# Down projections of a two-layer decoder step: where the residual rows, the first pair's weights and the last group's tiles are asked for

## The chip, the core and the metric

The kernel runs on one core of one Trainium2 chip. The metric is the time of one execution on the device in microseconds (us); before the change it is 2305.55 us, the median of three runs (2301.43, 2305.55 and 2307.38). Engines are called as the profile calls them: PE (TensorE's matmuls; PEld are its weight loads), DVE (VectorE), ACT (ScalarE), POOL (GpSimd) and SP (SyncE), which here only issues DMAs, one after the other in a fixed order.

## The reference, cut to what matters

A decoder of two layers works on 1024 prompt rows and 64 sample rows, 1088 columns in the kernel's layout (features lie on the partitions). Each layer is a mixer and a gated feed-forward block (FFN), and the change lies in the end of the FFN, its down projection:

```python
def _conv_ffn(h, buf, w_up, conv_w, conv_b, w_down):
    z = h @ w_up
    zc, new_buf = _causal_dwconv(z, buf, conv_w, conv_b)
    g, u = jnp.split(zc, 2, axis=-1)
    return (jax.nn.gelu(g) * u) @ w_down, new_buf
...
        y, fb = _conv_ffn(hn, ffn_buf[l], p['w_ffn_up'][l], p['ffn_conv_w'][l], p['ffn_conv_b'][l], p['w_ffn_down'][l])
        new_ffn.append(fb.astype(x.dtype))
        x = x + y
```

`w_ffn_down` is 2816 x 1024: 22 tiles of 128 inner features and 8 tiles of 128 output features. The last line is the residual add.

## The kernel before, in words

Every fp32 product is made of three matmuls on two-part numbers: each operand is split into a high part (made by ACT, a rounding copy) and a low part (made by DVE, value less high part), and PE adds high x high, high x low and low x high (`mm3`).

The residual `X` (8 rows of 128 x 1088, one row for each output tile) is written to DRAM ahead of the FFN (`self.spill`, "spf" in the profile), because the FFN's up projection uses the place of `X` for its own rows: four rows `Zs`, two rows `Ys` and the product row `YG`. The 22 finished inner tiles go to DRAM too (`yd`). The down projection fetches both again. It has three groups of inner tiles, `GROUPS = (6, 8, 8)`:

- **Group 0** (tiles 0 to 5) lies in the buffer `HX` and is multiplied directly: `first_block(w, m, o, n)` makes output tile m for a block of columns, on one of five PSUM banks, and DVE adds it to the residual row. Tiles m = 0, 1, 2 go block by block, then m = 3 and 4, each over the three blocks `TB`; then m = 5, 6, 7 together over the four blocks `QB` of 136 columns in either half. So PE has left the columns 0 to 271 of `HX` (the first two of the four blocks) half way through that last part. For each block `first_block` fetches the residual's piece from DRAM into a buffer of the pool `tmpp` ("xr").
- **Group 1** (tiles 6 to 13) is multiplied by a seven-product scheme: output tiles in four pairs (m, m + 4), seven products a pair on sums and differences of the operands. Columns go in two blocks, here called the first halves (columns 0 to 271 of either half of the row, `sb` = 0) and the second halves (272 to 543, `sb` = 1). In a pair PE makes four products of the first halves (`dfour`), four of the second, then the three others of each (`dthree`); in the first pair it makes all seven of the first halves and then all seven of the second. Products read by turns from `HB` and from `HX`. `into_hb(k, sb)` fills `HB` (one fetched tile each); `into_hx(k, sb)` fills `HX` for k = 0 to 3 from two fetched tiles y and z: three subtractions or additions on DVE (L727 to L729), then high and low parts (L712 and L713). `HX` still holds group 0, so `into_hx(k, 0)` must wait until PE has left those columns there, `into_hx(k, 1)` until group 0 ends. The seven weights of a pair are made by ACT and DVE from two fetched raw tiles; `W.make()` makes the next one of the seven (`Pair.steps`, L190 to L208). They lie in a pool of ten places, six of which the tiles 5 to 7 of group 0 hold to their end.
- **Group 2** (tiles 14 to 21) is multiplied directly from `HB` again, tile m = 0 over the blocks `TB`. `fetch(f, sb, hi, lo)` brings a tile's half into a buffer of `tmpp` and splits it into `HB` (L638 to L640), once the seven-product scheme has left that part of `HB`; `last(sb)` calls it during the last pair's `dthree`.

What sets the order: `tmpp` has four buffers, which go round among the pieces "xr" and the fetched tiles "yl". A DMA into a buffer is issued by SP when the buffer's last user has ended, and all DMAs stand in one SP queue, so a DMA that waits for a buffer holds back all behind it. A scheduler places the instructions of each engine ahead of time; each engine then takes its own in that order.

Of the kernel before, what the change touches and what calls it, by code (L numbers as in the profile page):

```python
# [11 lines left out]
ALU = mybir.AluOpType  # L12
# [3 lines left out]
KD = 8  # L16
# [72 lines left out]
def hybrid_step(ctx: ExitStack, tc: tile.TileContext, I, O):  # L89
    nc = tc.nc  # L90
# [16 lines left out]
    X = big.tile([P, KD, NT], F32, name="X")  # L107
# [57 lines left out]
    def get_w(key, ahead=4):  # L165
        i = state["next"]
        assert ORDER[i] == key, (ORDER[i], key)
        state["next"] += 1
        load_to(i + 1 + ahead)
        return wtiles.pop(i)  # L170
# [79 lines left out]
    def mm3(out, w_hi, w_lo, x_hi, x_lo, start, stop, more=False):  # L250
        mm(out, w_hi, x_hi, start, False, more)
        mm(out, w_hi, x_lo, False, False, more)
        mm(out, w_lo, x_hi, False, stop, more)
# [11 lines left out]
    def halves(ap, o, n):  # L265

        if len(ap.shape) == 2:
            return ap.rearrange("p (h c) -> p h c", h=2)[:, :, o:o + n]
        return ap.rearrange("p k (h c) -> p k h c", h=2)[:, :, :, o:o + n]

    def mm_halves(w, acts, o, n):

        ps = mmp.tile([P, 512], F32, tag="mm", name="mm")
        out = ps[:, :2 * n].rearrange("p (h c) -> p h c", h=2)
        for k, (hi, lo) in enumerate(acts):
            mm3(out, w[k][:, 0], w[k][:, 1], halves(hi, o, n), halves(lo, o, n), k == 0, k == len(acts) - 1)
        return out

    def blocks(w):
        return [t[:, :, k] for t in w for k in range(4)]  # L280
# [159 lines left out]
    HACTS = [(HH[:, k], HL[:, k]) for k in range(KD)]  # L440
# [40 lines left out]
    class FFN:  # L481
# [22 lines left out]
        def run(self, norm_next, final):  # L504
# [7 lines left out]
            c = 4 * NE  # L512
# [7 lines left out]
            v = nc.vector  # L520

            AF_ = [HX[:, e].rearrange("p q k c -> p (q k c)") for e in (0, 1)]
            AACTS = [tuple(a[:, q * NT:(q + 1) * NT] for a in AF_) for q in range(GROUPS[0])]
# [109 lines left out]
            def fetch(f, sb, hi, lo):  # L633

                o, n = SB[sb]
                t = tmpp.tile([P, 576], F32, tag="tmp", name="yl")
                tv = t[:, :2 * n].rearrange("p (h c) -> p h c", h=2)
                nc.sync.dma_start(tv, halves(self.yd[f], o, n))  # L638
                nc.scalar.activation(halves(hi, o, n), tv, AF.Copy)
                v.tensor_tensor(halves(lo, o, n), tv, halves(hi, o, n).bitcast(F32), ALU.subtract)  # L640

            W = self.first
            W.make(8)
            flush_all_but_last()
            for p in range(NFF):
# [8 lines left out]
                def make(i):  # L654
                    if nxt:
                        nxt.make()

                def make_first(i):
                    if i < 3:
                        make(i)  # L660

                def last(sb):
                    def go(i):
                        if not nxt and sb == 0:
                            q = i - 4
                            fetch(q, 0, *AACTS[q])
                        elif not nxt:
                            for q in {4: (3,), 5: (), 6: (4, 5)}[i]:
                                fetch(q, 0, *AACTS[q])
                    return go  # L670
# [15 lines left out]
                W = nxt  # L686
# [8 lines left out]


            def first_block(w, m, o, n):
                t = tmpp.tile([P, 576], F32, tag="tmp", name="xr")
                tv = t[:, :2 * n].rearrange("p (h c) -> p h c", h=2)
                nc.sync.dma_start(tv, self.spill[:, m, :, o:o + n])  # L700
                ps = mm_halves(blocks(w), AACTS, o, n)
                v.tensor_tensor(halves(X[:, m], o, n), tv, ps, ALU.add)

            def rows(f, sb):
                o, n = SB[sb]
                t = tmpp.tile([P, 576], F32, tag="tmp", name="yl")
                tv = t[:, :2 * n].rearrange("p (h c) -> p h c", h=2)
                nc.sync.dma_start(tv, halves(self.yd[f], o, n))
                return tv

            def put(hi, lo, src):
                nc.scalar.activation(hi, src, AF.Copy)  # L712
                v.tensor_tensor(lo, src, hi.bitcast(F32), ALU.subtract)  # L713

            G0, G1 = GROUPS[0], GROUPS[0] + GROUPS[1]

            def into_hb(k, sb):
                o, n = SB[sb]
                y = rows(G0 + k, sb)
                if k < 4:  # L720
                    v.tensor_tensor(y[:, 1], y[:, 1], y[:, 0], ALU.subtract)  # L721
                put(halves(HH[:, k], o, n), halves(HL[:, k], o, n), y)

            def into_hx(k, sb):
                o, n = SB[sb]
                y, z = rows(G0 + k, sb), rows(G0 + 4 + k, sb)
                v.tensor_tensor(y[:, 1], z[:, 1], y[:, 1], ALU.subtract)  # L727
                v.tensor_tensor(y[:, 0], y[:, 0], y[:, 1], ALU.add)
                v.tensor_tensor(z[:, 0], z[:, 0], y[:, 0], ALU.subtract)  # L729
                put(HX[:, 0, 0:2, k, o:o + n], HX[:, 1, 0:2, k, o:o + n], y)  # L730
                put(HX[:, 0, 2, k, o:o + n], HX[:, 1, 2, k, o:o + n], z[:, 0])

            def dn_pair(m):
                return Pair(self.up, [(key, (1, m)), (key, (1, m + 4))])

            todo = [(k, sb) for sb in (0, 1) for k in range(KD)]
            ws = [get_w((key, (0, m)), ahead=3 - m) for m in range(3)]
            for b in range(3):
                for m in range(3):
                    first_block(ws[m], m, *TB[b])  # L740
                    if b and todo:
                        into_hb(*todo.pop(0))
            for m in (3, 4):
                w = get_w((key, (0, m)), ahead=3)
                for b in range(3):
                    first_block(w, m, *TB[b])
                    into_hb(*todo.pop(0))
            ws = [get_w((key, (0, m)), ahead=KD - 1 - m) for m in (5, 6, 7)]
            W = dn_pair(0)
            for b in range(4):  # L750
                for w, m in zip(ws, (5, 6, 7)):
                    first_block(w, m, *QB[b])
                    if b < 2:
                        if todo:
                            into_hb(*todo.pop(0))
                    elif m > 5:
                        into_hx(2 * (b - 2) + m - 6, 0)
                    if b:
                        W.make({1: 1, 2: 0, 3: 0}[b])
            assert not todo  # L760
            W.make()
            for k in range(4):
                into_hx(k, 1)
                W.make()
# [29 lines left out]
            def dthree(m, W, sb, after):  # L794
                o, n = SB[sb]
                for i, ps, r, c in zip((4, 5, 6), xb.pop(sb), (m, m + 4, m), (o, o, NH + o)):
                    product(W.w[i], i, sb, ps, False)
                    xm = X[:, r, c:c + n]
                    v.tensor_tensor(xm, xm, ps[:, :n], ALU.add)
                    after(i)  # L800

            pair[0] = 1
            for m in range(4):
                nxt = dn_pair(m + 1) if m < 3 else None

                def make(i):
                    if nxt:
                        nxt.make()

                def make_first(i):  # L810
                    if i < 3:
                        make(i)

                def last(sb):
                    def go(i):
                        if nxt:
                            return
                        if sb == 0:
                            for q in (2 * (i - 4), 2 * (i - 4) + 1):
                                if q < 4:  # L820
                                    fetch(G1 + q, 0, *HACTS[q])
                        elif i < 6:
                            for q in (2 * i - 4, 2 * i - 3):
                                fetch(G1 + q, 0, *HACTS[q])
                    return go

                if m:
                    dfour(m, W, 0, make_first)
                    dfour(m, W, 1, make)
                    if not nxt:  # L830
                        load_to(state["next"] + 1)
                    dthree(m, W, 0, last(0))
                    dthree(m, W, 1, last(1))
                else:
                    dfour(m, W, 0, nothing)
                    W.make(8)
                    dthree(m, W, 0, nothing)
                    dfour(m, W, 1, make)
                    dthree(m, W, 1, make)
                W = nxt  # L840
            for q in range(KD):
                fetch(G1 + q, 1, *HACTS[q])

            def down(w, acts, t):
# [7 lines left out]
            for m in range(4):  # L852
                w = get_w((key, (2, m)), ahead=3)
# [678 lines left out]
```

## Time and profile before

| | before |
|---|---|
| median of three runs | 2305.55 us |
| the profiled execution, its time | 2306.45 us |
| its span, first to last instruction | 2304.7 us |
| mean granted TensorE clock | 0.987 |
| PE busy | 2249.4 us, 98% of the span |
| DVE busy | 1758.2 us, 76% |
| ACT busy | 1051.4 us, 46% |
| first layer: group 0, group 1 | 964.7 to 1036.5, 1036.5 to 1132.0 us |
| second layer: group 0, group 1 | 2028.4 to 2100.3, 2100.3 to 2195.5 us |

How to read it: a busy PE is not a PE at its peak, since the ends of matmuls are modelled; a wait shorter than a matmul hides in the busy time, and so does a lowered clock. Stages are therefore best measured from start to start of the same instruction. A row of the timeline has start, length, engine, line, operation, what it writes and reads, how many of the kind, and in brackets the idle time ahead of it and what ended that. A row of the busy times by stretch has the stretch, its length, then busy time and count of PE, PEld, DVE, ACT and POOL, the granted clock, the busy share of the DMA engines and GB/s.

### The profile page before, as it was taken

What the parts mean: (1) busy time and instruction counts of PE and PEld (TensorE: products, weight loads), DVE (VectorE), ACT (ScalarE), POOL (GpSimd) and SP (SyncE); (2) the same over time, 40 slices, a digit from 0 to 9 for tenths busy, and PEclk for the clock granted to TensorE, in tenths of its full rate; (3) what the DMA queues carried; (4) which work ended last, traced back from release to release, by engine and by line L of the source; (5) the groups of instructions that cost most, each with busy time, mean ns of one, the idle gap of its engine ahead of it and who ended that gap; (6) DMA issues with size and microseconds to landing.
All of it is one profiled execution on the core that took longest, in us unless ns stands there. A gap on an engine that the chain in (4) does not pass through costs nothing.

```text
span 2304.7 us, 39660 instructions
## 1 busy us (share of the span) xinstructions
PE 2249.4 (98%) x15992; PEld 2215.4 (96%) x15992; DVE 1758.2 (76%) x3185; ACT 1051.4 (46%) x2144; POOL 36.1 (2%) x65
## 2 busy tenths in 40 slices
PE   9999999989999999998999999998999999998998
PEld 8999998979999999998999999998999999998998
DVE  6899975698888888858737766589888888876745
ACT  6344437445444444523425766434444444533322
POOL 0000000000000000000000121000000000000000
PEclk9999999989999999999999999998999999999999
DMA  5212113212222122464422111322221222265312
GB/s 197 70 39 69 44 55 106 74 58 95 85 85 79 63 84 82 145 175 140 134 74 105 38 37 46 120 79 74 99 81 62 84 85 75 68 219 156 116 59 78
DMA packets 135288, 209.39 MB, mean 91 GB/s; under 512 B 27776, under 2 KB 101888, under 8 KB 134976
## 3 DMA queue, kind: packets, MB, share of 16 engines
q1 hardware_dynamic: 135104, 206.85, 28.3%
q8 instruction: 125, 2.05, 0.4%
q14 instruction: 59, 0.48, 0.1%
HBM read 160.62 MB, written 46.21 MB: 90 GB/s over the span
## 4 chain that ended last, share of the span: by engine, by line
PE 88%; DVE 6%; DMA 3%; ACT 2%; issue 1%; SPq 0%; DVEq 0%; ACTq 0%
PE mm L245 67%; PE ax L245 17%; DMA yl<-yd 2%; DVE acc L371 1%; DVE xe L1261 0%; PE ax L1376 0%; PE ax L1061 0%; DVE ws L160 0%; DVE ws L190 0%; PE ax L1052 0%; DMA X<-in_x 0%; DVE td L411 0%; DVE HB L406 0%; PE ax L1043 0%; PE ax L1023 0%
## 5 line engine op out<-in xcount | busy, mean ns | idle before, releaser
L245 PE MATMUL mm<-HB,ws 128*128 128x272 f32 (+6 forms) x9000 | 1405.0, 310 | 9.0 <-ACT HB L405 2.9
L245 PEld LDWEIGHTS mm<-HB,ws 128*128 128x128 f32 x9000 | 1330.5, 190 | 21.4 <-issue 6.7
L245 PE MATMUL mm<-HX,ws 128*128 128x272 f32 (+3 forms) x2844 | 411.6, 298 | 15.0 <-ACT HX L712 11.4
L245 PEld LDWEIGHTS mm<-HX,ws 128*128 128x128 f32 x2844 | 392.5, 191 | 17.3 <-ACT HX L712 12.3
L124 ACT ACTIVATE ws<-raw 128x512 fp32r<-128x512 f32 x484 | 296.3, 619 | 241.4 <-PE mm L245 113.2
L190 DVE TENSOR_TENSOR ws<-raw,ws 128x512 fp32r<-128x512 f32 x312 | 213.8, 688 | 77.4 <-ACT ws L124 75.0
L245 PE MATMUL ax<-HX,ws 128*128 128x272 f32 (+1 forms) x1872 | 265.1, 290 | 0.8 <-ACT HX L712 0.8
L245 PEld LDWEIGHTS ax<-HX,ws 128*128 128x128 f32 x1872 | 247.6, 189 | 1.6 <-ACT HX L712 1.3
L245 PE MATMUL ax<-HB,ws 128*128 128x272 f32 (+1 forms) x1248 | 171.6, 287 | 0.0
L245 PEld LDWEIGHTS ax<-HB,ws 128*128 128x128 f32 x1248 | 161.8, 188 | 0.0
L929 DVE SCALAR_TENSOR_TENSOR X<-U,par,X 128x1024 f32<-128x1024 f32 x120 | 151.7, 1279 | 0.0
L160 DVE TENSOR_TENSOR ws<-raw,ws 128x512 fp32r<-128x512 f32 (+1 forms) x172 | 110.8, 663 | 49.9 <-ACT ws L124 49.3
L607 ACT ACTIVATE X<-mm 128x272 f32<-128x272 f32 (+1 forms) x88 | 35.1, 398 | 189.6 <-PE mm L245 189.6
L620 DVE SCALAR_TENSOR_TENSOR X<-X,par 128x1104 f32<-128x1104 f32 x88 | 120.1, 1365 | 0.5 <-ACT X L619 0.4
L621 DVE SCALAR_TENSOR_TENSOR X<-X,par 128x1104 f32<-128x1104 f32 x88 | 116.5, 1364 | 0.0
L619 ACT ACTIVATE X<-X,par 128x1104 f32<-128x1104 f32 x88 | 114.2, 1298 | 0.2
L287 DVE TENSOR_TENSOR X<-X,mm 128x384 f32<-128x384 f32 (+1 forms) x66 | 34.6, 530 | 77.8 <-PE mm L245 69.4
L626 ACT ACTIVATE X<-X 128x1024 f32<-128x1024 f32 x44 | 46.6, 1060 | 45.5 <-DVE X L621 45.5
L551 ACT ACTIVATE X<-fst 128x16 f32<-128x16 f32 x88 | 17.9, 212 | 98.6 <-DVE X L621 98.6
L303 ACT ACTIVATE sq<-X 128x384 f32<-128x384 f32 (+1 forms) x42 | 20.7, 504 | 85.0 <-DVE X L287 79.2
L629 DVE TENSOR_TENSOR X<-X 128x1024 f32<-128x1024 f32 x44 | 53.6, 1219 | 0.4
L712 ACT ACTIVATE HB<-yl 128x544 fp32r<-128x544 f32 x32 | 21.0, 658 | 72.1 <-DVE yl L721 41.4
(262 smaller groups left out, 2079.6 us busy)
## 6 DMA issues: line engine op xcount, KB each, us to landing
raw<-in_w SPq DMA_DIRECT2D x176, 512.0 KB, 4.0
yl<-yd SPq DMA_DIRECT2D x120, 272.0 KB, 3.6
yd<-X SPq DMA_DIRECT2D x44, 544.0 KB, 2.7
raw<-in_w SPq DMA_DIRECT2D x16, 384.0 KB, 4.3
spf<-X SPq DMA_DIRECT2D x4, 1152.0 KB, 5.7
xr<-spf SPq DMA_DIRECT2D x20, 208.0 KB, 3.1
X<-in_xt SPq DMA_DIRECT2D x8, 512.0 KB, 6.7
spf<-X SPq DMA_DIRECT2D x4, 1024.0 KB, 5.3
```

Source lines behind the costliest of these rows:

```text
L124: nc.scalar.activation(hi, src, AF.Copy)
L160: nc.vector.tensor_tensor(lo, src, hi.bitcast(F32), ALU.subtract)
L190: nc.vector.tensor_tensor(lo, src, hi.bitcast(F32), ALU.subtract)
L245: nc.tensor.matmul(out, lhsT, rhs, start=start, stop=stop, skip_group_check=more)
L287: nc.vector.tensor_tensor(X[:, m, t0:t0 + n], X[:, m, t0:t0 + n], ps[:, :n], ALU.add)
L607: nc.scalar.activation(low(z1, sb), p1[:, :n], AF.Copy)
L619: nc.scalar.activation(y, z[:, 2:NE], AF.Identity, bias=pc(fb, f), scale=pc(fw, 2 * 44 + f))
L620: v.scalar_tensor_tensor(y, z[:, 1:NE - 1], pc(fw, 44 + f), y, ALU.mult, ALU.add)
L621: v.scalar_tensor_tensor(y, z[:, 0:NE - 2], pc(fw, f), y, ALU.mult, ALU.add)
L626: nc.scalar.activation(YG[:, :NP], y[:, :NP], AF.Gelu_apprx_tanh)
L629: v.tensor_tensor(YG[:, :NP], YG[:, :NP], y[:, :NP], ALU.mult)
L929: nc.vector.scalar_tensor_tensor(cv, U[i][:, j:j + NP], wj, cv, ALU.mult, ALU.add)
```

## The change

Three edits, all in `FFN.run`, so both layers have them.

1. The residual rows of output tiles 3 to 7 no longer pass through `tmpp`. Five DMAs fetch whole rows straight into `X` (rows 3 and 4 at the second block of the tiles 0 to 2, rows 5 to 7 at the third), and `first_block` adds the product to `X` in place. The pieces "xr" stay for m = 0, 1, 2: nine for each layer where there were 27.
2. The first pair's weights: of the eight calls of `W.make()`, two now stand at block 1, one at block 2 and one at block 3 of the tiles 5 to 7, and four with the second halves. Before, three stood at block 1, one behind block 3 and four with the second halves.
3. Group 2: four half tiles (0 to 3 of the second halves) are fetched during the last pair's `dthree` instead of behind it, two at each of its ends.

```diff
             def first_block(w, m, o, n):
+                if m > 2:
+                    ps = mm_halves(blocks(w), AACTS, o, n)
+                    v.tensor_tensor(halves(X[:, m], o, n), halves(X[:, m], o, n), ps, ALU.add)
+                    return
                 t = tmpp.tile([P, 576], F32, tag="tmp", name="xr")
...
             for b in range(3):
+
+                for m in ((), (3, 4), (5, 6, 7))[b]:
+                    nc.sync.dma_start(X[:, m].rearrange("p (h c) -> p h c", h=2), self.spill[:, m])
                 for m in range(3):
...
                     first_block(w, m, *QB[b])
-                    if b < 2:
-                        if todo:
-                            into_hb(*todo.pop(0))
-                    elif m > 5:
+                    if todo:
+                        into_hb(*todo.pop(0))
+                    elif b == 1 or m == 5:
+                        W.make()
+                    else:
                         into_hx(2 * (b - 2) + m - 6, 0)
-                    if b:
-                        W.make({1: 1, 2: 0, 3: 0}[b])
             assert not todo
-            W.make()
...
-                        if sb == 0:
-                            for q in (2 * (i - 4), 2 * (i - 4) + 1):
-                                if q < 4:
-                                    fetch(G1 + q, 0, *HACTS[q])
-                        elif i < 6:
-                            for q in (2 * i - 4, 2 * i - 3):
-                                fetch(G1 + q, 0, *HACTS[q])
+
+                        for q, c in ({4: ((0, 0), (1, 0)), 5: ((2, 0), (3, 0)), 6: ((0, 1), (1, 1))},
+                                     {4: ((4, 0), (5, 0)), 5: ((6, 0), (7, 0)), 6: ((2, 1), (3, 1))})[sb][i]:
+                            fetch(G1 + q, c, *HACTS[q])
...
-            for q in range(KD):
+            for q in range(4, KD):
                 fetch(G1 + q, 1, *HACTS[q])
```

The lines behind the first edit stand four lines later in the changed kernel.

SP's queue of the first layer at the end of group 0, where `into_hx` for k = 0 to 3 fetches its first halves; "yd_6" to "yd_9" are its tiles y, "yd_10" to "yd_13" its tiles z. Before:

```order
L700 DMA xr<-spf_3606 128x2x136
L708 DMA yl<-yd_13_3620 128x2x272
L700 DMA xr<-spf_3606 128x2x136 x4
L708 DMA yl<-yd_6_3613 128x2x272
L708 DMA yl<-yd_10_3617 128x2x272
L700 DMA xr<-spf_3606 128x2x136
L708 DMA yl<-yd_7_3614 128x2x272
L708 DMA yl<-yd_11_3618 128x2x272
L700 DMA xr<-spf_3606 128x2x136 x2
L708 DMA yl<-yd_8_3615 128x2x272
L708 DMA yl<-yd_12_3619 128x2x272
```

and now:

```order
L712 DMA yl<-yd_13_3620 128x2x272
L712 DMA yl<-yd_6_3613 128x2x272
L712 DMA yl<-yd_10_3617 128x2x272
L712 DMA yl<-yd_7_3614 128x2x272
L712 DMA yl<-yd_11_3618 128x2x272
L712 DMA yl<-yd_8_3615 128x2x272
L712 DMA yl<-yd_12_3619 128x2x272
```

The pieces of the residual are gone from between the tiles; the queue there holds tiles alone.

DVE of the first layer at the second halves of group 1 (L727 to L729, now L731 to L733, are the three operations of `into_hx`; "HX<-yl,HX" its low parts; "ws" and "raw" the weights of a pair). Before, from the operations of k = 0 on:

```order
L727 TENSOR_TENSOR yl<-yl 128x272
L778 TENSOR_TENSOR X<-X,mm 128x272
L728 TENSOR_TENSOR yl<-yl 128x272
L782 TENSOR_TENSOR X<-X,mm 128x272
L729 TENSOR_TENSOR yl<-yl 128x272
L713 TENSOR_TENSOR HX<-yl,HX 128x2x272
L713 TENSOR_TENSOR HX<-yl,HX 128x272
L786 TENSOR_TENSOR fst<-fst,mm 128x272
```

and now, to the last low part of k = 3:

```order
L198 TENSOR_TENSOR raw<-raw 128x512
L731 TENSOR_TENSOR yl<-yl 128x272
L190 TENSOR_TENSOR ws<-s_11155,ws 128x512
L732 TENSOR_TENSOR yl<-yl 128x272
L731 TENSOR_TENSOR yl<-yl 128x272
L733 TENSOR_TENSOR yl<-yl 128x272
L732 TENSOR_TENSOR yl<-yl 128x272
L717 TENSOR_TENSOR HX<-yl,HX 128x2x272
L717 TENSOR_TENSOR HX<-yl,HX 128x272
L733 TENSOR_TENSOR yl<-yl 128x272
L717 TENSOR_TENSOR HX<-yl,HX 128x2x272
L717 TENSOR_TENSOR HX<-yl,HX 128x272
```

Before, the second halves stand among the adds of the first pair's products (L778 to L799); now all four are done ahead of the fourth product's add (L791), with the second pair's first weights between them. PE's order follows: the first pair's matmuls stand in whole products of twelve, where before pieces of one to nine matmuls of several products were mixed.

SP's queue of the first layer around group 2 ("yd_14" to "yd_21" are tiles 0 to 7 of that group, each fetched once for the first halves and once for the second). Before:

```order
L129 DMA raw<-in_w 128x1024 x7
L638 DMA yl<-yd_18_3625 128x2x272
L638 DMA yl<-yd_19_3626 128x2x272
L638 DMA yl<-yd_20_3627 128x2x272
L638 DMA yl<-yd_21_3628 128x2x272
L129 DMA raw<-in_w 128x1024 x2
L638 DMA yl<-yd_14_3621 128x2x272
L638 DMA yl<-yd_15_3622 128x2x272
L638 DMA yl<-yd_16_3623 128x2x272
```

and now:

```order
L129 DMA raw<-in_w 128x1024 x7
L638 DMA yl<-yd_14_3621 128x2x272
L638 DMA yl<-yd_15_3622 128x2x272
L638 DMA yl<-yd_18_3625 128x2x272
L638 DMA yl<-yd_19_3626 128x2x272
L129 DMA raw<-in_w 128x1024
L638 DMA yl<-yd_20_3627 128x2x272
L638 DMA yl<-yd_21_3628 128x2x272
```

Two of the second halves have moved ahead of the last four first halves; two fewer are left for the end.

## Prediction

> **What bounds the kernel now.** First the chain that ended last, by engine (the page's part 4), then the busy times by stretch around the down projections.
>
> ```profile
> PE 88%; DVE 6%; DMA 3%; ACT 2%; issue 1%; SPq 0%; DVEq 0%; ACTq 0%
> ...
> 964.70:1036.50 71.80, 71.80 (x488) 71.55 (x487) 44.03 (x81) 22.93 (x41) 0.00 (x0) 1.00 0.62 182
> 1036.50:1132.00 95.50, 88.62 (x675) 87.41 (x674) 75.83 (x155) 34.02 (x62) 0.14 (x2) 0.95 0.43 131
> ...
> 2100.30:2195.50 95.20, 88.17 (x674) 87.35 (x673) 75.53 (x154) 33.75 (x62) 0.00 (x0) 0.95 0.44 131
> ...
> 1089.80:1110.90 21.10, 21.10 (x171) 21.10 (x170) 13.51 (x27) 5.11 (x9) 0.00 (x0) 1.00 0.15 51
> ```
>
> PE sets the end, so only PE's stops count. Group 0 has none. Group 1 has, at a clock of 0.95, while its third pair (last row) runs for 21.1 us without a gap. PE's timeline shows where:
>
> ```profile
> 1009.75 26.95 PE L245 MATMUL mm<-HX,ws 128*128 128x272 f32 x213
> ...
> 1036.53 1.67 PE L245 MATMUL mm<-HB,ws 128*128 128x272 f32 x12
> 1038.04 0.54 PE L245 MATMUL mm<-HX,ws 128*128 128x272 f32 x3
> 1039.38 0.39 PE L245 MATMUL mm<-HX,ws 128*128 128x272 f32 x1 [0.80 <-ACT HX L712]
> 1040.62 0.53 PE L245 MATMUL mm<-HX,ws 128*128 128x272 f32 x2 [0.85 <-DVE HX L713]
> ...
> 1045.93 0.59 PE L245 MATMUL mm<-HX,ws 128*128 128x272 f32 x1 [4.40 <-ACT HX L712]
> ...
> 1131.97 7.62 PE L245 MATMUL mm<-HB,ws 128*128 128x416 f32 x39
> 1140.25 0.45 PE L245 MATMUL mm<-HB,ws 128*128 128x416 f32 x1 [0.67 <-ACT HB L639]
> 1141.19 19.07 PE L245 MATMUL mm<-HB,ws 128*128 128x416 f32 x118 [0.48 <-DVE HB L640]
> ```
>
> Group 1's first product from `HB` runs, its second needs `HX`, which isn't there. Later group 2 stops once more, for its last tiles in `HB`. The long stop costs more than itself, as the clock by stretches of 2 us shows (the last number but two):
>
> ```profile
> 1040.00:1042.00 2.00, 0.90 (x5) 0.68 (x5) 2.00 (x5) 0.01 (x1) 0.00 (x0) 0.88 0.60 144
> 1042.00:1044.00 2.00, 0.00 (x0) 0.00 (x0) 1.38 (x3) 1.42 (x3) 0.00 (x0) 0.50 0.78 216
> ...
> 1050.00:1052.00 2.00, 2.00 (x11) 2.00 (x11) 2.00 (x5) 0.23 (x1) 0.00 (x0) 0.56 0.38 134
> ...
> 1140.00:1142.00 2.00, 1.26 (x5) 0.85 (x6) 1.93 (x6) 1.29 (x3) 0.00 (x0) 1.00 0.68 265
> ```
>
> A mean of 0.88 over 2 us is a clock that halves about 0.5 us before their end, at 1041.5; 0.56 is one that returns 1.8 us in, at 1051.8. PE runs again from 1045.93, so 5.8 us pass at half speed and 2.9 us are lost. In the short stop of group 2 (last row) the clock stays at 1.
>
> Why `HX` is late stands in the timeline of all engines:
>
> ```profile
> 1022.12 5.24 SPq L700 DMA_DIRECT2D xr<-spf  x4
> ...
> 1027.45 1.18 SPq L708 DMA_DIRECT2D yl<-yd  x2
> ...
> 1031.81 0.44 DVE L727 TENSOR_TENSOR yl<-yl 128x272 f32<-128x272 f32 x1 [2.50 <-DMA yl<-yd]
> ...
> 1032.81 0.98 ACT L712 ACTIVATE HX<-yl 128x544 fp32r<-128x544 f32 x2 [7.11 <-DVE yl L728]
> ...
> 1033.50 1.08 DVE L713 TENSOR_TENSOR HX<-yl,HX 128x544 fp32r<-128x544 f32 x2
> 1033.58 1.19 SPq L708 DMA_DIRECT2D yl<-yd  x2
> ...
> 1034.50 0.43 DVE L702 TENSOR_TENSOR X<-xr,mm 128x272 f32<-128x272 f32 x1
> ...
> 1039.25 0.69 DVE L190 TENSOR_TENSOR ws<-raw,ws 128x512 fp32r<-128x512 f32 x1
> ```
>
> SP spends 1022 to 1027 on four pieces "xr", each waiting for a buffer; only then come the tiles of k = 0, and those of k = 1 six microseconds later. PE had left the first columns of `HX` in the middle of the first row of its timeline: 1009.75 + (1036.53 - 1009.75) / 2 = 1023.1. So buffers are the limit, not data, DVE or PE.
>
> **What there is to gain.** Group 1 of the first layer takes 1131.97 - 1036.53 = 95.4 us, four pairs at 21.1 us would take 84.4: 11.0 us are lost. Of these 6.1 are the three waits shown, 2.9 the halved clock, and about 2.0 are waits too short to be named. The second layer:
>
> ```profile
> 2100.30 1.67 PE L245 MATMUL mm<-HB,ws 128*128 128x272 f32 x12
> ...
> 2195.52 8.99 PE L245 MATMUL mm<-HB,ws 128*128 128x416 f32 x45
> ...
> 2205.57 58.84 PE L245 MATMUL mm<-HB,ws 128*128 128x416 f32 x356 [0.30 <-DVE HB L640]
> ```
>
> 2195.52 - 2100.30 - 84.4 = 10.8 us. Group 2's stop: 40 matmuls from 1131.97 to 1141.19 at 7.62 / 39 = 0.195 us each would take 7.8 of the 9.2 us, so 1.4 us are lost; in the second layer 46 x 0.195 = 9.0 of 10.05, so 1.1 us. Together 11.0 + 10.8 + 1.4 + 1.1 = 24.3 us, the most this change can give.
>
> **Edit 1, the residual rows.** It removes 18 DMAs "xr" in each layer and their hold on the four buffers. DVE's adds stay (0.43 us, in place). The tiles of k = 0 and 1 can now lie in the buffers, subtracted, ahead of 1023.1. From there I work the queue on, with these landing times: the medians of the whole page (first row) and of the stretch 1020 to 1050, and the spread over all tiles that line L708 fetches.
>
> ```profile
> raw<-in_w SPq DMA_DIRECT2D x176, 512.0 KB, 4.0
> ...
> yl<-yd SPq DMA_DIRECT2D x11, 272.0 KB, 3.5
> raw<-in_w SPq DMA_DIRECT2D x2, 512.0 KB, 5.8
> ...
> DMA to landing us min/median/max: 3.0/3.5/6.2
> ```
>
> *First halves.* After 1023.1 the parts of k = 0 and 1 need 2 x 1.08 us on DVE, so by 1025.5 four buffers are free. SP issues k = 2 and 3 at once; they land 3.5 us later, at 1029. Two times three operations (0.44) and two low parts (1.08) make 4.8 us: done at about 1033.5. PE asks at 1038.0. The first stop goes, with 4.5 us to spare.
>
> *Second halves.* PE makes seven products in 21.1 / 2 = 10.55 us, to 1047.1, then one from `HB` (1.5), then at 1048.6 the product from `HX`; k = 3's low part is its eleventh matmul of twelve, at 1049.8. DVE's order has 33 instructions from 1033.5 to that part: eight on weights (0.69), twelve of `into_hx` (0.44), four pairs of low parts (1.08), five adds (0.43), together 5.5 + 5.3 + 4.3 + 2.2 = 17.3 us. If DVE never waits that is 1050.8, 1.0 us late; in the best case neighbours overlap and it is in time. It may also wait. The second pair's raw tile goes out near 1036.5, when a weight of the first pair gives its place free, and lands 4.0 to 5.8 us later, at 1040.5 to 1042.3; DVE has it in its order ahead of k = 1's last parts, and k = 3's tiles are fetched only into the buffers that these release, at 1042.5 to 1045. With 3.5 us of landing and some 3 us of DVE (three operations, two pairs of low parts partly beside the load) k = 3 is ready at 1049 to 1051.7. So it is 0 to 1.9 us late in each layer; I take 1.0, where the plain sum of DVE lies. At that length the clock should hold, as it did at 1140. Behind the waiting product stands all else that PE has, since its order is strict now.
>
> *The start.* Rows 3 and 4 of `X` lie where `Zs` and `Ys` were, rows 6 and 7 where `YG` is; in SP's queue they stand ahead of tiles and of pieces "xr" that used to go earlier.
>
> ```profile
> 973.71 0.53 SPq L708 DMA_DIRECT2D yl<-yd  x1
> ...
> 974.18 0.24 ACT L627 ACTIVATE X<-X 128x64 f32<-128x64 f32 x1
> ...
> 975.81 0.33 SPq L631 DMA_DIRECT2D yd<-X  x1
> ...
> yd<-X SPq DMA_DIRECT2D x1, 544.0 KB, 5.1
> ```
>
> SP now waits for ACT's last read (974.4), issues two rows and the store (976.2), and only then the tile of 973.71: 2.5 us later. Rows 6 and 7 wait for the store to land, 975.8 + 5.1 = 980.9. A block of 18 matmuls at 416 columns takes PE 18 x 0.195 = 3.5 us, so the pieces queued there serve adds of blocks that end from 964.7 + 5 x 3.5 = 982 on; and with five PSUM banks PE may be four blocks, 14 us, ahead of the adds. That covers it. Cost taken as nothing; without the cover 2.5 us a layer. It can't gain, as PE has no gap there. The bytes are the same: five rows of 544 KB either way.
>
> **Edit 2, the weights.** The fifth weight of the first pair was finished at 1039.9 (the L190 above); now it stands right behind k = 3's first halves, near 1034. PE names no wait for a weight, so the gain by itself is 0; it takes 0.69 us from DVE ahead of the second halves rather than behind, counted above. The pool's ten places allow four weights before tile 5 of group 0 ends, so three remain late, needed at 1042.5 and after.
>
> **Edit 3, group 2.** Two half tiles instead of four are fetched after the last ones' buffers come free. The timeline of SP before:
>
> ```profile
> 1127.96 3.12 SPq L638 DMA_DIRECT2D yl<-yd  x4
> ...
> 1132.58 4.55 SPq L638 DMA_DIRECT2D yl<-yd  x4
> ```
>
> Four in 4.55 us: the first two are out by about 1135, land 3.5 later at 1138.5 and are split at 1140.6 at the latest (a pair takes ACT 0.98 and DVE 1.08, the rows above). PE reaches the eighth tile 24 + 21 matmuls of 0.195 after 1131.97, at 1140.7. The stop goes; between 0 and 0.5 us may stay in each layer, I take 0.
>
> **The sum.** 24.3 - 2 x 1.0 = 22.3 us. 2306.45 - 22.3 = 2284.2; the median of the runs lies 0.9 below the profiled execution, so 2283.
>
> **Rivals.**
> - *The second halves come late enough to close the clock again.* The landing times reach 6.2 us, 2.7 over the median; with two such loads behind one another k = 3 is more than 4 us late. Then PE loses what it loses now at one long stop, 4.4 + 2.9 = 7.3 us a layer: 2283 + 2 x (7.3 - 1.0) = 2295.6, or 2289 in one layer alone. For it: the DMA engines were 0.60 and 0.78 busy in the 2 us rows at 1040 and 1042. Against: four buffers free of "xr". The Trainium skill, "TensorE: Matmul & The Clock Gate", section "What's actually happening", has the array's clock halved after an idle window of about 3.4 us and restored after about as long a busy one. The trace agrees on the fall, about 3.5 us after the stops began, though PE was not wholly idle; the return took 5.8 us. By the page's window the half-speed run would cost an estimated 1.7 us, and this rival would end at 2293.
> - *The stop only moves.* DVE is busy 75.8 of 95.5 us in group 1; if its order, not the buffers, holds `HX` back, PE stands at the second halves as long as it did at the first: 8 + 2.9 us a layer, about 2305. Against: DVE sat idle 2.5 us and ACT 7.1 us for the very first tiles.
> - *Slower.* SP, held by rows 6 and 7, which must wait for `YG`'s store, brings the pieces "xr" of blocks 1 and 2 so late that PE runs out of PSUM banks. It decides beyond 14 us of delay, and must cost over 24.3 + 7 us in all to end slower: some 30 us of delay a layer, 16 uncovered, 2306.45 + 32 - 24.3 - 0.9 = 2313. Against: a store of 5.1 us.
>
> **How the numbers follow.** The forecast 0.72, the clock rival 0.19, the moved stop 0.07, the queue 0.02. The forecast's own range is 2281 (nothing late) to 2285 (1.9 each), with the scatter of the runs shown (4.1 below, 1.8 above the median) 2277 to 2287. To leave out no more than 2 in 10 it goes up through the clock rival in one layer and most of it in both: 2277 to 2294. About 0.3%, 6.9 us, is what a measurement of this kernel can tell from no change: faster are the first two cases, 0.91; same 0.07; slower 0.02.
>
> **What would show it.** Right: group 1 takes 84.4 to 87 us in both layers; no PE wait of over 2 us on `HX`; the clock stays at 1.0 through group 1; SP issues the first halves of k = 0 and 1 before PE has left their columns; group 2's first 48 matmuls run through. Wrong: a wait at the eighth or ninth product of the first pair with a clock of 0.5 behind it, any PE gap in group 0, or PE waiting for "ws".

## The result and the profile after

The changed kernel takes 2285.16 us (median of four runs: 2285.22, 2285.74, 2285.1 and 2283.69) and the kernel before 2304.67 us (four runs, 2301.43 to 2307.38). The ratio is 0.9915, with a 95% interval of 0.9898 to 0.9932: 15.7 to 23.5 us less, 19.5 by the medians. 2283 us was predicted, with a range of 2277 to 2294. The profiled execution took 2285.22 us, its span is 2283.1 us.

The chain that ended last (the page's part 4) holds more of PE and less of DMA:

```profile
PE 91%; DVE 5%; ACT 2%; DMA 1%; issue 1%; DVEq 0%; SPq 0%; ACTq 0%
```

The busy times by stretch of group 1 in both layers (stretch, length, busy time and count of PE, PEld, DVE, ACT and POOL, the granted clock, DMA share, GB/s):

```profile
1039.00:1123.30 84.30, 84.30 (x674) 84.30 (x673) 67.35 (x135) 30.40 (x56) 0.14 (x2) 1.00 0.40 123
2090.80:2175.10 84.30, 84.30 (x675) 84.30 (x674) 66.90 (x133) 29.63 (x55) 0.00 (x0) 1.00 0.40 123
```

PE is busy all through, the clock is 1.00, and the length is four pairs at 21.1 us. PE's timeline shows the places where it stood before:

```profile
967.14 72.04 PE L245 MATMUL mm<-HX,ws 128*128 128x416 f32 x486
1039.02 1.67 PE L245 MATMUL mm<-HB,ws 128*128 128x272 f32 x12
1040.52 1.66 PE L245 MATMUL mm<-HX,ws 128*128 128x272 f32 x12
...
1051.09 1.67 PE L245 MATMUL ax<-HX,ws 128*128 128x272 f32 x12
...
1123.34 8.83 PE L245 MATMUL mm<-HB,ws 128*128 128x416 f32 x46
1132.59 12.70 PE L245 MATMUL mm<-HB,ws 128*128 128x416 f32 x80 [0.43 <-DVE HB L640]
...
2018.90 72.04 PE L245 MATMUL mm<-HX,ws 128*128 128x416 f32 x486
2090.78 1.67 PE L245 MATMUL mm<-HB,ws 128*128 128x272 f32 x12
...
2175.09 40.13 PE L245 MATMUL mm<-HB,ws 128*128 128x416 f32 x241
```

Group 0 goes over into group 1 without a gap; the first product from `HX` (1040.52) and the first one of the second halves (1051.09) run as whole products of 12. Group 1 takes 1123.34 - 1039.02 = 84.32 and 2175.09 - 2090.78 = 84.31 us. Of group 2's stops one of 0.43 us is left in the first layer, none in the second. From start to start, group 2's first 48 matmuls (its two blocks of 416 columns) take 9.74 and 9.06 us, where they took 10.98 and 10.54 before: 1.2 and 1.5 us less.

Where the time came from: from group 0's start in the first layer to its start in the second it was 2028.4 - 964.7 = 1063.7 us and is 2018.90 - 967.14 = 1051.8, so 11.9 less. From there to the end of the span it was 2304.7 - 2028.4 = 276.3 and is 2283.1 - 2018.9 = 264.2, so 12.1 less. Together 24.0 us. The code ahead of 967.14, which the change leaves alone, took 2.4 us more in this execution; the clock stood at 0.50 for 23.9 us there, against 17.1 in the execution of before. So the spans differ by 21.6.

The timeline of the other engines, with what the prediction had worked out by the queue:

```profile
976.61 1.38 SPq L745 DMA_DIRECT2D X<-spf  x2
979.16 0.32 SPq L631 DMA_DIRECT2D yd<-X  x1
979.53 0.53 SPq L712 DMA_DIRECT2D yl<-yd  x1
...
988.31 1.02 SPq L745 DMA_DIRECT2D X<-spf  x2
...
1019.08 0.45 DVE L731 TENSOR_TENSOR yl<-yl 128x272 f32<-128x272 f32 x1
...
1022.19 0.44 DVE L731 TENSOR_TENSOR yl<-yl 128x272 f32<-128x272 f32 x1 [1.01 <-DMA yl<-yd]
...
1024.48 1.85 ACT L716 ACTIVATE HX<-yl 128x544 fp32r<-128x544 f32 x4 [5.49 <-PE mm L245]
...
1029.97 0.44 DVE L731 TENSOR_TENSOR yl<-yl 128x272 f32<-128x272 f32 x1 [1.65 <-DMA yl<-yd]
...
1034.25 1.08 DVE L717 TENSOR_TENSOR HX<-yl,HX 128x544 fp32r<-128x544 f32 x2
...
1048.30 0.43 DVE L733 TENSOR_TENSOR yl<-yl 128x272 f32<-128x272 f32 x1
...
1048.65 0.43 DVE L732 TENSOR_TENSOR yl<-yl 128x272 f32<-128x272 f32 x1
...
1050.34 1.07 DVE L717 TENSOR_TENSOR HX<-yl,HX 128x544 fp32r<-128x544 f32 x2
```

The tiles of k = 0 and 1 (1019.08 and 1022.19) are in the buffers before PE leaves the columns. ACT now waits for PE (5.49 us), where before it waited for tiles and what DVE makes of them. The first halves end with k = 3's low parts at 1035.3, 5.2 us ahead of PE's first product from `HX`; the second halves at 1051.4.

### The profile page after: what moved, and what is told of

Read it like the earlier page. It is cut to its first block, busy times and chain, and to the rows that moved or that the text cites. A ratio compares the mean times of both kernels' runs of the same rounds, so it can differ in the third digit from the quotient of the medians.

```text
span 2283.1 us, 39594 instructions
## 1 busy us (share of the span) xinstructions
PE 2241.2 (98%) x15992; PEld 2210.9 (97%) x15992; DVE 1759.1 (77%) x3185; ACT 1051.0 (46%) x2144; POOL 36.2 (2%) x65
## 4 chain that ended last, share of the span: by engine, by line
PE 91%; DVE 5%; ACT 2%; DMA 1%; issue 1%; DVEq 0%; SPq 0%; ACTq 0%
PE mm L245 69%; PE ax L245 17%; DVE acc L371 1%; PE ax L1378 0%; DVE xe L1263 0%; PE ax L1063 0%; DMA yl<-yd 0%; PE ax L1054 0%; DMA X<-in_x 0%; DVE td L411 0%; DVE HB L406 0%; PE ax L1025 0%; PE ax L1013 0%; PE ax L1045 0%; DVE X L1298 0%
## 5 line engine op out<-in xcount | busy, mean ns | idle before, releaser
L245 PE MATMUL mm<-HX,ws 128*128 128x272 f32 (+3 forms) x2844 | 405.5, 296 | 1.9 <-DVE X L595 1.9
L610 DVE TENSOR_TENSOR X<-X,mm 128x272 f32<-128x272 f32 (+1 forms) x44 | 19.2, 437 | 45.1 <-PE mm L245 45.1
```

The lines of the kernel that those rows point to most:

```text
L245: nc.tensor.matmul(out, lhsT, rhs, start=start, stop=stop, skip_group_check=more)
```

## The experiments

The groups of each profiled execution, start to start of the same instruction, and the medians. The kernel before was run again beside each group of kernels, with medians of 2304.67 to 2306.43 us; the ratios are taken against those runs. Group 1 is that of one execution: the kernel before and the second edit alone have the same order of instructions, and yet their group 1 differs by 3.2 us over both layers.

| kernel | group 1, first and second layer, us | median, us | ratio to before, 95% interval |
|---|---|---|---|
| before | 95.4, 95.2 | 2304.67 | |
| changed | 84.3, 84.3 | 2285.16 | 0.9898 to 0.9932 |
| first edit alone | 84.3, 84.3 | 2287.45 | 0.9901 to 0.9928 |
| second edit alone | 95.3, 92.2 | 2304.34 | 0.9988 to 1.0007 |
| third edit alone | 93.4, 94.0 | 2301.70 | 0.9973 to 0.9991 |
| pieces, but into X | 85.2, 84.3 | 2287.29 | 0.9901 to 0.9928 |
| rows 5 to 7 alone | 87.7, 88.7 | 2294.58 | 0.9928 to 0.9967 |
| rows 3 and 4 alone | 92.9, 92.2 | 2302.17 | 0.9967 to 0.9988 |
| rows 6 and 7 alone | 93.8, 91.3 | 2304.66 | 0.9983 to 1.0002 |
| changed, 6 repeats on DVE | 87.3, 85.8 | 2287.34 | 0.9906 to 0.9935 |
| changed, 9 repeats | 87.6, 86.0 | 2287.15 | 0.9906 to 0.9936 |
| changed, 12 repeats | 87.4, 87.2 | 2288.69 | 0.9911 to 0.9945 |

### Each edit alone

**The first edit.** The kernel before, with the diff's first two pieces only.

> The kernel before with the first edit alone: rows 3 to 7 of the residual straight into X, so that the pieces of tiles 3 to 7 leave the four buffers. Theory (the buffers held HX back): group 1 takes 84.3 us in both layers, the clock stays at 1.0 there, and the stop of group 2 stays as before (1.4 and 1.1 us); 24.1 - 2 x 1.2 = 21.7 us less than before, about 2283 us. Rival (the weights made sooner carry the gain, or are needed for it): group 1 keeps part of its 11 us and the time is above 2290 us.

Measured: 2287.45 us, 17.8 below the runs of before beside it (16.6 to 22.8 at the ends of the interval). PE's timeline of this kernel:

```profile
1037.69 1.67 PE L245 MATMUL mm<-HB,ws 128*128 128x272 f32 x12
...
1122.01 7.50 PE L245 MATMUL mm<-HB,ws 128*128 128x416 f32 x39
1129.98 0.46 PE L245 MATMUL mm<-HB,ws 128*128 128x416 f32 x1 [0.48 <-ACT HB L639]
1130.91 14.26 PE L245 MATMUL mm<-HB,ws 128*128 128x416 f32 x88 [0.47 <-DVE HB L640]
```

1122.01 - 1037.69 = 84.32: the stop in group 1 is gone, the one in group 2 is still there. The median is 4 us higher than expected, inside the interval.

**The second edit.** The kernel before with `W.make()` called as in the changed kernel:

```diff
-                    if b < 2:
-                        if todo:
-                            into_hb(*todo.pop(0))
-                    elif m > 5:
+                    if todo:
+                        into_hb(*todo.pop(0))
+                    elif b == 1 or m == 5:
+                        W.make()
+                    else:
                         into_hx(2 * (b - 2) + m - 6, 0)
```

> The kernel before with the second edit alone, the calls of W.make() moved. The order of instructions comes out the same as before on all five engines: the scheduler puts the weights where it did. Theory: no change, within 0.3 per cent of before, group 1 at 95.4 us in both layers. Rival (the weights carry the gain): over 7 us less. If the time differs by more than 2 us from before, that is the measurement's own scatter, since the two programs are one.

Measured: ratio 0.9998. The edit does nothing at all, as the scheduler gives the same order of instructions with it and without it. PE stands as before:

```profile
1040.09 0.54 PE L245 MATMUL mm<-HB,ws 128*128 128x272 f32 x3
1045.16 0.59 PE L245 MATMUL mm<-HX,ws 128*128 128x272 f32 x1 [4.53 <-ACT HX L712]
```

Yet group 1 took 95.3 us in one layer and 92.2 in the other, in one execution of one program. How much of that is the clock is told below.

**The third edit.** The kernel before with the diff's last two pieces only.

> The kernel before with the third edit alone, four half tiles of group 2 fetched during the last pair. Theory: group 1 stays at 95.4 us, the stop of group 2 goes from 1.4 and 1.1 us to 0 to 0.5 us in each layer, so 1.5 to 2.5 us less than before. Rival (the tiles collide with the last pair's own transfers or with DVE's work there): the last pair gets longer than 21.1 us and nothing is gained, or some us are lost.

Measured: 2301.70 us, 3.6 less (2.1 to 6.2). In its trace group 2 keeps a stop of 0.37 us in the first layer and none in the second. Its first 48 matmuls take 9.69 and 9.06 us, so 1.3 and 1.5 us are gone, 2.8 in all, a little more than expected. Group 1 was also 2.0 and 1.2 us shorter in this execution, with the same stop on `HX` (4.51 us in the first layer), about as much as one order of instructions scatters. The rival falls: the last pair takes 21.08 us in both layers, as before.

The two edits that work add up: 17.8 + 3.6 = 21.4, against the change's 19.5 (15.7 to 23.5).

### Buffers or transfers

`first_block` still asks for 18 pieces in each layer, but each lands in its place in `X`:

```diff
+                if m > 2:
+                    xm = halves(X[:, m], o, n)
+                    nc.sync.dma_start(xm, halves(self.spill[:, m].rearrange("p h c -> p (h c)"), o, n))
+                    v.tensor_tensor(xm, xm, mm_halves(blocks(w), AACTS, o, n), ALU.add)
+                    return
```

> The kernel before, with the residual of tiles 3 to 7 still fetched in 18 pieces a layer and still asked for piece by piece, but each piece lands in its place in X instead of in one of the four buffers, and the product is added there. The number of transfers is that of before, the buffers are free as in the changed kernel. Theory (the buffers are the limit): group 1 at 84.3 to 85 us in both layers, all of the first edit's 21.7 us. Rival (the number of transfers in SP's queue is the limit, some 0.3 us to issue each): 18 x 0.3 = 5 us of SP time a layer stay, HX stays late by some of it, and group 1 takes 88 us or more.

Measured: 2287.29 us, as with whole rows. So it is the four buffers, and not the number of transfers. In the second layer group 1 is 84.3 us. In the first there is one short stop:

```profile
1048.40 1.42 PE L245 MATMUL ax<-HX,ws 128*128 128x272 f32 x10
1050.39 0.52 PE L245 MATMUL ax<-HX,ws 128*128 128x272 f32 x2 [0.58 <-DVE HX L718]
```

That is the eleventh matmul of the ninth product, the very place where the prediction let the second halves come late.

### Which pieces

Rows 5 to 7 alone come straight into `X`, whose pieces stood among the tiles of the first halves:

```diff
-                if m > 2:
+                if m > 4:
-                for m in ((), (3, 4), (5, 6, 7))[b]:
+                for m in ((), (), (5, 6, 7))[b]:
```

> The kernel before with a part of the first edit: only the rows of tiles 5 to 7 come straight into X; tiles 3 and 4 keep their pieces in the four buffers. The pieces that stood between the first halves' tiles were those of tiles 5 to 7. Theory: they alone held HX back, so group 1 takes 84.3 to 85.2 us in both layers and the time is about 21 us below before, as with rows 3 to 7. Rival (rows 3 and 4 are needed too, because the pieces delay all that stands behind them in the queue): HX comes late by the queue's delay and group 1 stays above 88 us.

Measured: 2294.58 us, 11.4 less than before, half as much as expected. The rival was nearer: rows 3 and 4 are needed too. But group 1 is at 87.7 and 88.7 us and not above 88 in both layers, and it isn't the first halves that come too late. The timeline:

```profile
1032.05 0.44 DVE L731 TENSOR_TENSOR yl<-yl 128x272 f32<-128x272 f32 x1 [2.63 <-DMA yl<-yd]
...
1036.84 1.67 PE L245 MATMUL mm<-HB,ws 128*128 128x272 f32 x12
...
1045.81 0.43 DVE L785 TENSOR_TENSOR X<-X,mm 128x272 f32<-128x272 f32 x1
...
1046.30 1.78 PE L245 MATMUL mm<-HX,ws 128*128 128x272 f32 x12 [1.78 <-DVE X L785]
...
1053.47 0.52 PE L245 MATMUL ax<-HX,ws 128*128 128x272 f32 x2 [0.70 <-DVE HX L717]
```

No product waits for the first halves any more. But k = 2's tile (L731) comes 4.8 us ahead of group 1, where it is 1039.02 - 1029.97 = 9.05 in the changed kernel. The six pieces of tiles 3 and 4 go through the same four buffers earlier on, so the last tiles for `HB` and then those for `HX` come later. All that DVE does for the second halves is 4 us late, the adds among it too: PE waits 1.78 us for an add that is to give a PSUM bank free (L785), then 0.70 us for k = 3.

The other part: `if m in (3, 4)`, and `((), (3, 4), ())`.

> The kernel before with the other part of the first edit: only the rows of tiles 3 and 4 come straight into X; tiles 5 to 7 keep their 12 pieces a layer in the four buffers. With rows 5 to 7 alone the gain was 11.4 of the first edit's some 18 to 22 us. If the parts add up, this gives the rest, 7 to 10 us. Theory now: the pieces of tiles 5 to 7 stand among the very tiles that PE waits for, and their buffers come free at PE's pace, so as long as they are there HX's first halves stay late, and an earlier queue ahead of them helps little: group 1 stays above 92 us in both layers, gain 0 to 5 us. On the clock, from the traces so far: it changes only on a grid of 3.41 us, falls at the end of a stretch of that grid in which PE did fewer than some 12 matmuls of 272 columns, and returns at the end of the first stretch in which it did 13 or more; so time at half speed is 3.4, 6.8 or 10.2 us.

And two of the three rows: `if m > 5`, and `((), (), (6, 7))`.

> The kernel before with the rows of tiles 6 and 7 alone straight into X; tiles 3 to 5 keep their pieces, so 4 pieces a layer (tile 5's) still stand among the tiles of the first halves. Theory: group 1 lies between that with rows 5 to 7 (87.7 and 88.7 us) and that of before (95.4), 88.5 to 94 us, and the time 4 to 11 us below before. Rival (any piece left in that place restores the whole stop): 95 us. The clock again falls and returns only on the grid of 3.41 us, falls with fewer than some 12 matmuls of 272 columns in a stretch, and stays at 1.0 with 14 or more.

Rows 3 and 4: 2302.17 us, 4.3 less than before (2.8 to 7.6). Rows 6 and 7: 2304.66 us, 1.8 less, no difference that can be told. The timeline with rows 3 and 4, where SP still stands at four pieces:

```profile
1021.51 5.28 SPq L704 DMA_DIRECT2D xr<-spf  x4
...
1046.68 0.59 PE L245 MATMUL mm<-HX,ws 128*128 128x272 f32 x1 [4.39 <-ACT HX L716]
```

The timeline with rows 6 and 7:

```profile
1020.82 9.40 SPq L712 DMA_DIRECT2D yl<-yd  x4
1030.40 0.46 SPq L704 DMA_DIRECT2D xr<-spf  x1
...
1046.48 0.59 PE L245 MATMUL mm<-HX,ws 128*128 128x272 f32 x1 [4.45 <-ACT HX L716]
```

In both the long stop is there, in the first layer at its full length (4.39 and 4.45 us, where it was 4.40). With rows 6 and 7 SP needs 9.4 us for the four tiles of k = 0 and 1, and a piece of tile 5 (1030.40) goes ahead of those of k = 2 and 3. Over both layers the changed kernel's group 1 is 22.0 us shorter than before. Rows 5 to 7 alone make it 14.3 us shorter and rows 3 and 4 alone 5.6, so these parts nearly add up; by the medians it is 11.4 and 4.3 of the first edit's 17.8.

With rows 6 and 7 the expectation is half met. Group 1, 93.8 and 91.3 us, lies in the 88.5 to 94 us that were expected, 5.5 us less than before over both layers; but that execution was the fastest of ten (2302.14 us). The time is 3.9 us less to 0.5 more than before, and not the 4 to 11 less that were expected. By the time the rival, that any piece left there brings the stop back, was nearer. By the medians the eight pieces of tiles 6 and 7 are worth 1.8 us, and tile 5's four, taken out next to these, 9.6 (11.4 - 1.8).

### The slack of the second halves

The changed kernel with a low part of k = 0 written six, nine or twelve times more:

```diff
                 put(HX[:, 0, 2, k, o:o + n], HX[:, 1, 2, k, o:o + n], z[:, 0])
+                if (k, sb) == (0, 1):
+                    hi, lo = HX[:, 0, 0:2, k, o:o + n], HX[:, 1, 0:2, k, o:o + n]
+                    for _ in range(6):
+                        v.tensor_tensor(lo, y, hi.bitcast(F32), ALU.subtract)
```

> The changed kernel with six repeats of one low part of k = 0, second halves, on DVE (0.72 us each, about 0.63 apart): the same value is written again, so only time is added, 3.8 us ahead of the second halves' last parts, which are 1.3 us early in the changed kernel. Theory of the prediction (DVE's chain of second halves is the next limit, with a slack of about 1 us, and a stop of under 3 us leaves the clock at 1.0): PE stops for about 2.5 us at the ninth product of group 1, no halved clock, group 1 at 86.5 to 87.5 us in both layers, time 5 us over the changed kernel. Rival (the slack is larger, as DVE's waits for tiles take up the delay): group 1 stays at 84.3 us.

> The same with nine repeats, 5.7 us of DVE. Theory: PE stops for 4.4 us, which is about what halved the clock before (a wait of 4.4 us behind shorter ones); group 1 at 84.3 + 4.4 = 88.7 us if the clock holds and 91.6 us if it halves for the 5.8 us that it did before. By the Trainium skill (TensorE: Matmul & The Clock Gate, What's actually happening), an idle window of about 3.4 us halves it, so the latter, with an estimated 1.7 us for the half speed in place of 2.9. Rival (the slack is larger): group 1 under 86 us.

> The same with twelve repeats, 7.6 us of DVE. Theory: PE stops for 6.3 us, the clock halves within the stop, about 3.5 us after its start, and stays at 0.5 for about 3 us or more after PE runs again: group 1 at 84.3 + 6.3 + 1.7 to 2.9 = 92.3 to 93.5 us in both layers, so the time is back at about 2303 us, the clock rival in full. Rival (the clock follows the share of work and not a window): no half speed, group 1 at 90.6 us.

The medians are 2.2, 2.0 and 3.5 us above the changed kernel's, which was run at another time; group 1 tells more. Six repeats, PE:

```profile
1046.47 1.76 PE L245 MATMUL mm<-HX,ws 128*128 128x272 f32 x12 [1.65 <-DVE X L787]
...
1053.34 0.52 PE L245 MATMUL ax<-HX,ws 128*128 128x272 f32 x2 [0.37 <-DVE HX L717]
```

3.0 and 1.5 us are lost in group 1, at the clock of 1.0. The first layer's 87.3 us is in the range of 86.5 to 87.5, the second's 85.8 below it, so the slack was a little larger than thought. In the first layer most is lost one step earlier than thought, at the PSUM bank; in the second 0.4 us there and 1.0 at the ninth product. With nine and twelve the forecast of 88.7 to 93.5 us fell. The scheduler knows of these repeats: with nine and twelve it moves products of PE ahead and the second pair's weights behind, so that no single stop is over 2 us. So these two don't measure what a stop of 4 to 6 us costs, and that the clock stayed at 1.0 in them says nothing against the clock rival. The stop of before was another kind: a wait in SP's queue for buffers, with PE's order standing still behind it.

## Why the prediction was right

- **The bound and the sum available.** Right in group 1: 11.0 + 10.8 us were named, 11.1 + 10.9 came back. Group 2's stops were put too low: 7.62 / 39 = 0.195 us a matmul has the last one's whole length in it. From start to start it is 9.06 / 48 = 0.189 us in the changed kernel's second layer, so the stops had cost 10.98 - 9.06 = 1.9 and 10.54 - 9.06 = 1.5 us, not 1.4 and 1.1, and 1.2 and 1.5 of that came back. That makes 24.7 us from the stages named; 24.0 are seen from group 0's start on, so the code beside these stages took 0.7 more.
- **Edit 1, the first halves.** Right in kind: with the buffers free the tiles of k = 0 and 1 wait for PE, no longer PE for them, and 5.2 us are to spare where 4.5 were worked out. But the prediction saw the cause too narrowly, in the four pieces of 1022 to 1027. Without these and the others of tiles 5 to 7, 14.3 of the 22.0 us of group 1 come back (by the medians 11.4 of 17.8); the pieces of tiles 3 and 4, earlier in the queue, hold the rest.
- **Edit 1, the second halves.** The term of the sum that was mis-sized: 1.0 us a layer was taken, nothing was lost. k = 3's low parts end at 1051.4, and of the ninth product from 1051.09 the eleventh matmul, which needs the first of them, comes 1.3 us on at 1052.3, after both have ended. The 33 durations of DVE were added to 17.3 us; the trace has 1051.4 - 1035.3 = 16.1, with waits of 0.76 in it (three of 0.16, 0.17 and 0.43), so the work itself took 15.3. In the rows shown, an instruction of 0.43 us at 1048.30 is followed by the next at 1048.65, 0.35 us on: durations overlap, and their sum was too long by an eighth. That the term is real, and near zero, is shown by the 0.58 us of the pieces kernel, the 0.70 of rows 5 to 7 and the 0.37 of six repeats, all at that matmul.
- **The start of group 0.** The tile behind the first two rows goes out at 979.53, 12.4 us after group 0's start, where it was 9.0: 3.4 us later and not 2.5. Rows 6 and 7 go at 988.31. PE has no gap, so the cost is nothing, as taken.
- **Edit 2.** Its worth of 0 was right, its working was wrong. The fifth weight stands earlier because of the first edit. The calls move no instruction of the kernel before; and the kernel with the first edit alone, which lacks them, has the same order as the changed one on PE, DVE, ACT and SP through groups 0 and 1.
- **Edit 3.** 0 was taken as left. It is 9.74 - 9.06 = 0.7 us in the first layer, with a stop of 0.43, and nothing in the second. So the sign that group 2's first 48 matmuls run through came in the second layer alone.
- **From the trace to the median.** 24.0 us less the 2.4 that the unchanged code ahead took more are 21.6. By medians it is 19.5, and the interval holds the 22.3 that was predicted. For the profiled execution 2284.2 us was worked out and 2285.22 measured. That these lie 1 us apart is in part luck: the gain behind group 0's start was 1.7 us larger than forecast, and the code ahead of it, for which no change was forecast, took 2.4 more.
- **The rivals.** The clock stays at 1.0 in group 1; the stop didn't move; SP's queue held rows 6 and 7 back for 21.2 us after group 0's start and PE didn't notice.

## What to carry to other kernels

Where small pieces and large tiles go round one pool and one DMA queue, look for the buffer that the queue waits for, and give the pieces a place that is free anyway: it was worth all of the long stop, while the same number of transfers did no harm. Removing only the pieces that stand at the stop gives back part of it, since those ahead delay all that follows. Durations of short DVE instructions overlap (0.43 us long and 0.35 apart here), so a chain is measured from start to start, and a scheduler may undo what a source line moves: look at the order before a term is written for it.

## What the runs showed of the hardware

The clock of PE changes on a fixed grid. In the profiled execution of before it changes, among other points, at 512.46, 1041.53 and 2106.49 us, which lie 155 and 312 times 3.4133 us apart. The stretches of 3.41 us here are laid on such points. The last number but two is the clock, the first count that of PE's matmuls. The kernel with rows 5 to 7, with a stop of 1.78 us in the first layer and one of 2.41 in the second:

```profile
1042.91:1046.32 3.41, 1.63 (x14) 1.41 (x13) 2.94 (x8) 1.61 (x3) 0.00 (x0) 1.00 0.89 263
1046.32:1049.74 3.42, 3.42 (x27) 3.42 (x28) 2.71 (x6) 0.63 (x1) 0.00 (x0) 1.00 0.73 241
2101.05:2104.46 3.41, 1.35 (x11) 1.13 (x10) 3.41 (x9) 1.60 (x3) 0.00 (x0) 1.00 0.78 247
2104.46:2107.87 3.41, 3.06 (x13) 3.06 (x14) 2.80 (x7) 0.64 (x2) 0.00 (x0) 0.50 0.89 265
2107.87:2111.29 3.42, 3.42 (x29) 3.42 (x28) 3.12 (x8) 1.67 (x3) 0.00 (x0) 1.00 0.11 38
```

The kernel with rows 6 and 7, first layer:

```profile
1040.49:1043.90 3.41, 1.30 (x9) 0.85 (x7) 3.41 (x7) 1.59 (x3) 0.00 (x0) 1.00 0.47 141
1043.90:1047.32 3.42, 0.83 (x3) 0.84 (x4) 2.08 (x6) 0.94 (x2) 0.00 (x0) 0.50 0.99 298
1047.32:1050.73 3.41, 2.30 (x10) 1.98 (x10) 3.41 (x9) 1.44 (x3) 0.00 (x0) 0.50 0.42 146
1050.73:1054.14 3.41, 3.41 (x17) 3.41 (x16) 2.16 (x5) 1.26 (x2) 0.00 (x0) 0.50 0.89 290
1054.14:1057.55 3.41, 3.41 (x29) 3.41 (x28) 3.14 (x8) 1.09 (x2) 0.00 (x0) 1.00 0.02 6
```

The kernel with the second edit alone, second layer, in which the half speed ends with the third stretch:

```profile
2099.26:2102.67 3.41, 1.41 (x12) 1.19 (x10) 2.78 (x6) 1.43 (x3) 0.00 (x0) 1.00 0.79 203
2102.67:2106.09 3.42, 0.58 (x2) 0.58 (x3) 2.69 (x6) 1.09 (x2) 0.00 (x0) 0.50 0.96 310
2106.09:2109.50 3.41, 3.41 (x17) 3.41 (x16) 2.67 (x6) 1.26 (x2) 0.00 (x0) 0.50 0.90 291
```

And two more: the kernel before, ahead of its fall in group 1 of the first layer, and the kernel with pieces into X, in group 2 of the first layer, where the matmuls have 416 columns:

```profile
1038.11:1041.53 3.42, 1.76 (x10) 1.11 (x8) 3.39 (x9) 1.09 (x2) 0.00 (x0) 1.00 0.30 75
1128.05:1131.47 3.42, 2.27 (x9) 1.18 (x8) 3.02 (x9) 3.01 (x5) 0.00 (x0) 1.00 0.85 269
```

A stretch is at 1.00 or at 0.50 from end to end. In group 1, whose matmuls have 272 columns, a stretch is followed by 0.50 if PE ran 12 matmuls or fewer in it, and by 1.00 if it ran 13 or more, whether it was itself at full or at half speed (27 to 30 are counted in a full stretch at 1.00, 16 or 17 at 0.50; at 1.00 the fewest seen to keep the clock are 14). A trace may lack a matmul or two. PE's busy time alone doesn't decide: 1.76 us with 10 matmuls was followed by 0.50 (before), 1.63 us with 14 by 1.00 (rows 5 to 7). Nor is the count itself the measure: nine matmuls of 416 columns were followed by 1.00. What is measured inside the chip stays open. The rule is read from group 1 in all traces here. The expectations of rows 3 and 4 and of rows 6 and 7 state it ahead of their runs, whose four falls and four returns all keep to it.

So a stop of 2.41 us halved the clock, and stops of 1.78 and 1.65 us did not. Half speed lasted 3.4, 6.8 or 10.2 us. The 5.8 us after the stop that the prediction read are the end of such a time of 10.2 us, which had begun inside the stop, at 1041.53. What half speed costs is half of the time in which PE works at it, and the grid has a part in that: in the second edit's run PE worked 6.2 us at 0.50 in the first layer and 4.0 in the second, so 3.1 and 2.0 us were lost. That is 1.1 of the 3.1 us by which the two layers differ (95.3 and 92.2). Another 1.3 are waits, 6.5 us in all against 5.2, since the first layer has one of 1.28 us ahead of the long one; 0.7 have no name. That the grid makes much of the scatter between the runs of before is possible, but wasn't tried.

The Trainium skill, "TensorE: Matmul & The Clock Gate", section "What's actually happening", gives a free-running window of 3413 ns; the grid above agrees with it. Its table there has the clock fall after an idle window; here a window with 12 matmuls, 1.41 us of work, was enough, and the measurement decides.
